# A two-layer hybrid decoder step: shared weight tiles, the convolution's halo in one go, roots on GpSimd, and an earlier q

## The chip, the cores and the metric

The kernel runs on one core of one Trainium2 chip. A core has five engines, each with its own queue that it works through in order: TensorE (PE, matmuls), VectorE (DVE), ScalarE (ACT), GpSimd (POOL) and SyncE (SP, which here issues all the DMAs). They wait for each other by semaphores. The metric is the device time of one launch in microseconds. The kernel before took 2385.9 us, the median of three runs (2383.13 to 2389.49).

## The reference

Each of two layers normalises its input, projects it by one weight matrix of 1024 x 2824, runs two groups of heads on the result, and adds the output projection of both to the input. It does so for a prompt of 2048 new tokens and for eight short samples of 4 tokens with caches.

```python
q = _rope(_rms(aq.reshape(B, L, ATT_HEADS, HEAD_DIM), q_norm_g), pos)     # 8 heads of 64
k = _rope(_rms(ak...), pos)                                               # 2 heads
att = _swa_banded(q, k, v, sinks)              # window of 128, softmax with a sink
att = att * jax.nn.silu(ag)
# delta branch: causal convolution over 4 tokens, 1536 channels
xx = jnp.concatenate([conv_buf, dqkv], 1)
y = silu(sum(xx[:, j:j + L] * conv_w[j] for j in range(4)))
q, k = _l2n(q) * 128 ** -0.5, _l2n(k)          # 4 heads of 128
beta, g = sigmoid(db), -exp(a_log) * softplus(da + dt_bias)
o, s_new = _gated_delta(q, k, v, beta, g, s0)  # per chunk: a triangular solve, then a scan
o = _rms(o, dn_norm_g) * jax.nn.silu(dg)
y = jnp.einsum('ble,ed->bld', jnp.concatenate([att, dn], -1), w_out)
return x + y, nk, nv, nbuf, ns
```

`_rms` and `_l2n` each need a reciprocal root of a sum of squares; the convolution needs the last three columns of the tokens before (the halo).

## The kernel before

**Tiling.** A layer is worked in four groups of 512 tokens (gi = 0 to 3), some 297 us each. A group runs all input projections as matmuls of 128 x 512 outputs, in blocks of four or eight weight pieces, one after the other in program order: k/v/gates, the delta branch's k (four tiles), attention q, delta q (four tiles), delta v (four tiles), the gates, then the output projection. Each product is done as three passes over halves (hi and lo) of weights and activations; all these matmuls are line L484.

**Weights.** In group 0 of a layer each piece comes in whole (`raw`, 128 x 512, from a ring of three slots), ACT writes its rounded half hi (L262), POOL the rest lo (L263), and SP stores both to DRAM; groups 1 to 3 load these. In group 0, and for the output weights in group 2, PE also multiplies the samples' rows by the raw piece (L519). The ring of split weights `hl` has five slots.

**Side tasks.** Everything else is a task, cut into steps, with a start and an end counted in projection steps: the table W. While a group's projections are written out, the tasks that are due put their steps in between: k's norm (`k1`), the q heads (`q0`, `q1`), the inversion of the triangular blocks on POOL (`ir0`, `ir1`: `inv_rows`, 31 rounds of L811 and L813, two instructions each), what follows from it on PE (`iv0`, `iv1`), attention (`att0`, `att1`), the delta scan (`sc0`, `sc1`), the samples' attention and delta (`sa`, `sp`, `sh`, in group 1). A scheduler then orders the instructions on each engine; within an engine they start in that order.

**Shared buffers.** Tiles of 4 KB a partition come from five slots (`f4`): among them the two q heads `qh`, the squares, At (the inversion's input, read back from DRAM by L805), X, and the scores Pt. Tiles of 2 KB come from nine slots (`f2`): th of each silu, the inversion's pr and Xh, PT, the output rows. A tile that takes a slot waits until the last reader of the tile before is done.

**q, attention.** L389 to L403 square, sum, take the root, multiply and rotate each of the two `qh`; L645 transposes them on PE, L649 and L650 split the result into q; L668 and L669 multiply by k; L672 (ACT) copies the product into Pt, L673 masks it; L689 is the exponential, L696 the normalisation, L701 the transposition of Pt on PE, L711 the product with v. L681 to L692 are the small steps between.

**Roots.** `rsqrt(out, x)` is a bit trick and three Newton steps on DVE: 11 small instructions (L200, L201, three times L203, L204, L205), on tiles of at most 128 x 16. It is called for x (xrs), k and the q heads (qr), the delta branch's k (sqvk) and q (rq), and its outputs (ro), and for the samples.

**Convolution.** `conv_tile` has one of 12 feature tiles (k, q, v) in a PSUM bank: ACT writes the last tap (L741), DVE adds the three others over the columns d to 511 (L744), each followed by the halo's 1 to 3 columns (L745), then copies the last three columns of the bank to `halo` (L746); `silu2` is a tanh on ACT (L210) and a product on DVE (L211). k and q tiles are KQ, v tiles vT, which PE transposes (L912).

Of the kernel before, what the change touches and what calls it, by code (L numbers as in the profile page):

```python
# [10 lines left out]
F32 = mybir.dt.float32  # L11
F32R = mybir.dt.float32r
BF16 = mybir.dt.bfloat16
I32 = mybir.dt.int32
AF = mybir.ActivationFunctionType
ALU = mybir.AluOpType
# [29 lines left out]

W = dict(k1=8, pre0=13, pre1=19, q0=17, q1=30, ir0=20, ir1=((32,) + (27,) * 3), iv0=(36, 31, 31, 31), iv1=(41, 36, 36, 36), att0=24, att1=47,
         qk0=29, qk1=35, sc0=(41,) * 4, sc1=52, sa0=-4, sa1=30, sp0=20, sp1=50, sh0=58, shd=11, shl=13, wla=4, wraw=3, xn0=2, xn1=8, sla=3,
         md0=53, md1=55, ma0=45)
# [92 lines left out]
def hybrid_kernel(ctx, tc, a):  # L142
# [23 lines left out]
    def f2(shape, dt=F32, name="f2"):  # L166
        return f2p.tile(shape, dt, tag="f2", name=name, bufs=9)

# [9 lines left out]
    def smt(shape, nm, bufs=2):  # L178
        return sm.tile(shape, F32, tag=nm, name=nm, bufs=bufs)
# [11 lines left out]
    trib, selb = tsb[:, 0:P], tsb[:, P:]  # L191
    cs_s = cp.tile([R3, S_END], F32, name="cs_s")
    junk = cp.tile([P, P], BF16, name="junk")
    negc = cp.tile([P, 1], F32, name="negc")

    def rsqrt(out, x):

        n, m = x.shape
        t = sm.tile([P, 16], F32, tag="rs_t", name="rs_t", bufs=2)[:n, :m]
        V.tensor_scalar(t.bitcast(I32), x.bitcast(I32), 1, None, op0=ALU.logical_shift_right)  # L200
        V.tensor_scalar(out.bitcast(I32), t.bitcast(I32), -1, 0x5F3759DF, op0=ALU.mult, op1=ALU.add)  # L201
        for _ in range(3):
            V.scalar_tensor_tensor(t, out, -0.5, x, op0=ALU.mult, op1=ALU.mult)  # L203
            V.tensor_mul(t, t, out)  # L204
            V.scalar_tensor_tensor(out, t, 1.5, out, op0=ALU.add, op1=ALU.mult)  # L205

# [40 lines left out]
    def fetch(first=False):  # L247


        while len(wready) < W["wla"]:  # L250
# [4 lines left out]
            with nullcontext() if first else tc.high_priority():  # L255
                raw = None
                if whole:
                    raw = wp.tile([P, kk, m], F32, tag="raw", name="raw", bufs=W["wraw"])
                    dma(raw, src)
                hl = wp.tile([P, 2, kk, m], F32R, tag="hl", name="hl", bufs=W["wla"] + 1)  # L260
                if split:
                    A.copy(hl[:, 0], raw)  # L262
                    G.tensor_sub(hl[:, 1], raw, hl[:, 0].bitcast(F32))  # L263
                else:
                    dma(hl.bitcast(F32), half)
# [276 lines left out]
    def group(L, gi, xT, sg):  # L542
# [11 lines left out]
        if gi > 0:  # L554
            V.tensor_copy(kT[:, :, 0:P], kT[:, :, NT * P:].bitcast(F32))
        vts = [L.vt]
        kall = f2([P, NT, 2, HD], name="kall")
# [182 lines left out]
        def conv_tile(ft, ps, dest):  # L740
            A.activation(dest, ps, AF.Copy, scale=convw[:, ft, 3:4])  # L741
            for d in range(1, 4):
                w = convw[:, ft, 3 - d:4 - d]
                V.scalar_tensor_tensor(dest[:, d:], ps[:, 0:T - d], w, dest[:, d:], op0=ALU.mult, op1=ALU.add)  # L744
                V.scalar_tensor_tensor(dest[:, 0:d], halo[:, ft, 3 - d:3], w, dest[:, 0:d], op0=ALU.mult, op1=ALU.add)  # L745
            V.tensor_copy(halo[:, ft, :], ps[:, T - 3:T])  # L746
            silu2(dest, dest, P, T)
# [513 lines left out]
    def sample_head(L, h):  # L1261
# [8 lines left out]
        dma(dg, zs[:, Z_DG + h * P:Z_DG + (h + 1) * P])  # L1270
        sel = f2([P, 2, P], name="sel")
        dma(sel, a["const_k"])
        yield
# [91 lines left out]
    dma(cst[:, P:], a["const"][:, P:])  # L1365
    dma(cs_s, a["const_s"])
    V.tensor_copy(identb, ident)
    tsf = f2([P, P + 16], name="tsf")
# [91 lines left out]
```

## Time and profile before

| | us |
|---|---|
| median of 3 runs | 2385.9 (2383.13 to 2389.49) |
| the profiled execution's own time | 2384.89 |
| its span in the trace | 2383.1 |
| PE busy | 2227.7 (93%), 14340 instructions |
| DVE busy | 1642.2 (69%), 5060 instructions |
| ACT busy | 909.6 (38%), 2864 instructions |
| POOL busy | 447.4 (19%), 732 instructions |
| mean granted TensorE clock | 0.972 of full |

A row of the profile names the line, engine and operation, the tile written and the tiles read (KQ<-mm,pc), the size, and behind it the time; "<-" behind an idle time names what ended it. PE rows are at full speed at a granted clock of 1.0 (2.4 GHz) and half of that at 0.5.

### The profile page before, as it was taken

How to read it: one execution, taken by the hardware profiler on the slowest of the kernel's cores; microseconds unless marked ns; L12 is line 12 of the kernel's file. 1: busy time of each engine (PE TensorE's matmuls, PEld its weight loads, DVE VectorE, ACT ScalarE, POOL GpSimd, SP SyncE). 2: the span in 40 equal slices, each digit the busy share in tenths (PEclk: the TensorE clock that was granted, in tenths of full speed). 3: DMA queues.
4: the chain of work that ended last, by engine and by line, in shares of the span. 5: the costliest groups of instructions: out<-in, count | busy, mean ns of one | idle time of the engine just before them, and what ended most of it. 6: DMA issues, size and time to landing. Idle time of an engine off the chain costs nothing.

```text
span 2383.1 us, 41057 instructions
## 1 busy us (share of the span) xinstructions
PE 2227.7 (93%) x14340; PEld 1771.6 (74%) x14340; DVE 1642.2 (69%) x5060; ACT 909.6 (38%) x2864; POOL 447.4 (19%) x732
## 2 busy tenths in 40 slices
PE   6989999879999899979999899999899989999799
PEld 5766788658887687867877677887688777788677
DVE  6677677577678764677656867778767787557663
ACT  3544523234233342334325445244432344323331
POOL 3272320400004000040023623104000130002100
PEclk9989999979999999989999999999999999999899
DMA  5654685514765348544566546854357534675236
GB/s 172 208 190 160 206 282 184 158 57 140 225 194 170 105 146 267 181 124 131 162 213 222 173 148 215 272 190 125 118 162 224 192 113 133 200 231 161 82 116 199
DMA packets 211298, 414.14 MB, mean 174 GB/s; under 512 B 61340, under 2 KB 89604, under 8 KB 211028
## 3 DMA queue, kind: packets, MB, share of 16 engines
q1 hardware_dynamic: 211092, 411.53, 53.4%
q8 instruction: 113, 1.85, 0.3%
q14 instruction: 93, 0.76, 0.1%
HBM read 312.84 MB, written 101.62 MB: 174 GB/s over the span
## 4 chain that ended last, share of the span: by engine, by line
PE 59%; DVE 8%; POOL 6%; DMA 3%; issue 2%; ACT 2%; SPq 0%; POOLq 0%; ACTq 0%; DVEq 0%
PE mm L484 40%; POOL Xh L813 3%; POOL pr L811 3%; PE px L711 2%; PE px L946 1%; PE px L954 1%; PE px L940 1%; PE px L926 1%; PE px L934 1%; PE px L701 1%; PE px L781 1%; DMA hl<-hl 1%; PE px L668 1%; PE px L519 1%; DVE vT L744 1%
## 5 line engine op out<-in xcount | busy, mean ns | idle before, releaser
L484 PE MATMUL mm<-xT,hl 128*128 128x512 f32 x3072 | 777.5, 403 | 4.1 <-POOL hl L263 3.8
L484 PEld LDWEIGHTS mm<-xT,hl 128*128 128x128 f32 x3072 | 571.0, 192 | 124.2 <-issue 6.7
L484 PE MATMUL mm<-hl,xT 128*128 128x512 f32 (+1 forms) x2304 | 511.2, 369 | 44.3 <-DVE rs_t L204 25.9
L484 PEld LDWEIGHTS mm<-hl,xT 128*128 128x128 f32 x2304 | 379.1, 192 | 114.4 <-issue 56.5
L263 POOL TENSOR_TENSOR hl<-raw,hl 128x512 fp32r<-128x512 f32 (+1 forms) x144 | 186.5, 1300 | 409.7 <-ACT hl L262 360.2
L811 POOL TENSOR_TENSOR pr<-At,Xh 128x126 f32<-128x126 f32 (+22 forms) x248 | 99.2, 400 | 580.1 <-DMA At<-ad 286.6
L484 PE MATMUL mm<-mixA,hl 128*128 128x512 f32 x768 | 187.9, 397 | 0.0
L484 PE MATMUL mm<-mixD,hl 128*128 128x512 f32 x768 | 181.6, 392 | 1.0 <-DVE mixD L970 1.0
L1029 POOL TENSOR_TENSOR mixA<-m,mixA 128x256 fp32r<-128x256 f32 x64 | 45.5, 736 | 719.2 <-ACT mixA L1028 492.7
L484 PEld LDWEIGHTS mm<-mixD,hl 128*128 128x128 f32 x768 | 142.6, 188 | 33.7 <-DVE mixD L970 1.8
L744 DVE SCALAR_TENSOR_TENSOR KQ<-mm,pc,KQ 128x511 f32<-128x511 f32 (+2 forms) x192 | 142.0, 740 | 35.1 <-ACT KQ L741 34.8
L484 PEld LDWEIGHTS mm<-mixA,hl 128*128 128x128 f32 x768 | 140.7, 188 | 30.4 <-issue 2.2
L262 ACT CAST hl<-raw 128x512 fp32r<-128x512 f32 (+1 forms) x144 | 85.0, 595 | 140.2 <-PE mm L484 76.4
L689 ACT ACTIVATE Pt<-Pt,nm 128x128 f32<-128x128 f32 x256 | 99.3, 391 | 21.5 <-DVE nm L681 21.5
L813 POOL TENSOR_TENSOR Xh<-Xh,pr 128x126 f32<-128x126 f32 (+22 forms) x248 | 103.0, 416 | 18.9
L1060 DVE TENSOR_TENSOR xr<-mm,xr 128x512 f32<-128x512 f32 x64 | 43.7, 691 | 79.6 <-PE mm L484 79.6
L672 ACT COPY Pt<-px 128x256 f32<-128x256 f32 x128 | 43.7, 374 | 143.1 <-PE px L669 110.8
L704 DVE TENSOR_TENSOR PT<-px,cst 128x512 f32<-128x512 f32 x124 | 82.1, 683 | 16.7 <-PE px L701 16.2
L701 PE MATMUL px<-cst,Pt 128*128 128x128 f32 x256 | 41.9, 289 | 41.2 <-ACT th L210 26.9
L741 ACT ACTIVATE KQ<-mm,pc 128x512 f32<-128x512 f32 x64 | 43.7, 687 | 94.0 <-PE mm L484 93.9
L668 PE MATMUL px<-kT,q 128*128 128x256 f32 (+1 forms) x256 | 72.6, 313 | 5.0 <-DVE q L650 1.7
L359 ACT CAST xT<-x 128x512 fp32r<-128x512 f32 x64 | 35.5, 618 | 93.9 <-PE mm L484 83.0
(392 smaller groups left out, 3708.7 us busy)
## 6 DMA issues: line engine op xcount, KB each, us to landing
hl<-hl SPq DMA_DIRECT2D x512, 512.0 KB
hl<-hl SPq DMA_DIRECT2D x64, 264.0 KB
raw<-in_wf_dram SPq DMA_DIRECT2D x64, 256.0 KB
raw<-in_w_out_dram SPq DMA_DIRECT2D x64, 256.0 KB
x<-in_x_prompt_dram SPq DMA_DIRECT2D x16, 512.0 KB
raw<-in_wt_dram SPq DMA_DIRECT2D x32, 256.0 KB
xr<-in_x_prompt_dram SPq DMA_DIRECT2D x32, 256.0 KB
y<-xr SPq DMA_DIRECT2D x32, 256.0 KB
```

Source lines behind the costliest of these rows:

```text
L262: A.copy(hl[:, 0], raw)
L263: G.tensor_sub(hl[:, 1], raw, hl[:, 0].bitcast(F32))
L484: PE.matmul(pss[u], lhs, rhs, start=(k == 0 and q == 0), stop=(k == 7 and q == 2))
L668: PE.matmul(sps[kv][:, jj, c0:], q, kT[:, kv, cols], start=True, stop=False)
L689: A.activation(Pt[:, kv, j], Pt[:, kv, j], AF.Exp, bias=nm[:, h:h + 1], scale=0.125, accum_out=den[:, h:h + 1])
L701: PE.transpose(pt[:, j, :], Pt[:, kv, j], ident)
L704: V.tensor_mul(ptt, pt, (umat if kb else slower).unsqueeze(1).to_broadcast([P, 4, P]))
L711: PE.matmul(po[kv * HD:kv * HD + HD, :], vts[tt + kb][:, kv * HD:kv * HD + HD], PT[kv, kb].rearrange("p a b -> p (a b)"), start=(kb == 0 o ...
L744: V.scalar_tensor_tensor(dest[:, d:], ps[:, 0:T - d], w, dest[:, d:], op0=ALU.mult, op1=ALU.add)
L811: G.tensor_mul(pr, At[:, j, j + 1:].unsqueeze(2).to_broadcast([P, n, m]), Xh[:, j, 0:m].unsqueeze(1).to_broadcast([P, n, m]))
L813: G.tensor_sub(Xh[:, j + 1:, 0:m], Xh[:, j + 1:, 0:m], pr)
L1029: G.tensor_sub(lo, m, hi.bitcast(F32))
```

## The change

Five edits.

- `raw` comes from the f2 ring. It has 12 slots now, and the ring of three raw slots is gone: the same memory.
- `rsqrt` is one GpSimd instruction, x to the power of -0.5, with a constant tile of -0.5 as its second operand.
- The halo's part of the convolution: at the start of a group (not of group 0, where the halo is zero) five small GpSimd instructions work out, for all twelve tiles, what the halo adds to the first three columns (`hc`); a tile's L745 three times becomes one DVE addition (L751). The copy of the last three columns is done by ACT (L749).
- q0, q1 go from 17, 30 to 18, 27: the q heads' six steps start one projection step later and end three sooner.
- The samples' constant `sel` is loaded once, in place of eight loads into an f2 tile.

```diff
-W = dict(k1=8, pre0=13, pre1=19, q0=17, q1=30, ir0=20, ir1=((32,) + (27,) * 3), iv0=(36, 31, 31, 31), iv1=(41, 36, 36, 36), att0=24, att1=47,
-         qk0=29, qk1=35, sc0=(41,) * 4, sc1=52, sa0=-4, sa1=30, sp0=20, sp1=50, sh0=58, shd=11, shl=13, wla=4, wraw=3, xn0=2, xn1=8, sla=3,
+W = dict(k1=8, pre0=13, pre1=19, q0=18, q1=27, ir0=20, ir1=((32,) + (27,) * 3), iv0=(36, 31, 31, 31), iv1=(41, 36, 36, 36), att0=24, att1=47,
+         qk0=29, qk1=35, sc0=(41,) * 4, sc1=52, sa0=-4, sa1=30, sp0=20, sp1=50, sh0=58, shd=11, shl=13, wla=4, xn0=2, xn1=8, sla=3,
...
     def f2(shape, dt=F32, name="f2"):
-        return f2p.tile(shape, dt, tag="f2", name=name, bufs=9)
+        return f2p.tile(shape, dt, tag="f2", name=name, bufs=12)
...
+    sel = cp.tile([P, 2, P], F32, name="sel")
+    mhalf = cp.tile([P, 16], F32, name="mhalf")
+    V.memset(mhalf, -0.5)
     def rsqrt(out, x):
         n, m = x.shape
-        t = sm.tile([P, 16], F32, tag="rs_t", name="rs_t", bufs=2)[:n, :m]
-        V.tensor_scalar(t.bitcast(I32), x.bitcast(I32), 1, None, op0=ALU.logical_shift_right)
-        V.tensor_scalar(out.bitcast(I32), t.bitcast(I32), -1, 0x5F3759DF, op0=ALU.mult, op1=ALU.add)
-        for _ in range(3):
-            V.scalar_tensor_tensor(t, out, -0.5, x, op0=ALU.mult, op1=ALU.mult)
-            V.tensor_mul(t, t, out)
-            V.scalar_tensor_tensor(out, t, 1.5, out, op0=ALU.add, op1=ALU.mult)
+        G.tensor_tensor(out, x, mhalf[:n, 0:m], op=ALU.pow)
...
-                    raw = wp.tile([P, kk, m], F32, tag="raw", name="raw", bufs=W["wraw"])
+                    raw = f2([P, kk, m], name="raw")
...
+        if gi > 0:
+            hc, ht = smt([P, 12, 3], "hc", 1), smt([P, 12, 2], "ht", 1)
+            G.tensor_mul(hc, halo, convw[:, :, 0:1].to_broadcast([P, 12, 3]))
+            for d in (2, 1):
+                G.tensor_mul(ht[:, :, 0:d], halo[:, :, 3 - d:], convw[:, :, 3 - d:4 - d].to_broadcast([P, 12, d]))
+                G.tensor_add(hc[:, :, 0:d], hc[:, :, 0:d], ht[:, :, 0:d])
...
         def conv_tile(ft, ps, dest):
             A.activation(dest, ps, AF.Copy, scale=convw[:, ft, 3:4])
             for d in range(1, 4):
-                w = convw[:, ft, 3 - d:4 - d]
-                V.scalar_tensor_tensor(dest[:, d:], ps[:, 0:T - d], w, dest[:, d:], op0=ALU.mult, op1=ALU.add)
-                V.scalar_tensor_tensor(dest[:, 0:d], halo[:, ft, 3 - d:3], w, dest[:, 0:d], op0=ALU.mult, op1=ALU.add)
-            V.tensor_copy(halo[:, ft, :], ps[:, T - 3:T])
+                V.scalar_tensor_tensor(dest[:, d:], ps[:, 0:T - d], convw[:, ft, 3 - d:4 - d], dest[:, d:], op0=ALU.mult,
+                                       op1=ALU.add)
+            A.copy(halo[:, ft, :], ps[:, T - 3:T])
+            if gi > 0:
+                V.tensor_add(dest[:, 0:3], dest[:, 0:3], hc[:, ft])
             silu2(dest, dest, P, T)
```

The order of instructions moves with it. Three places follow; lines of the new kernel have other numbers (L484 is L481, L263 L260, L672 L676, L689 L693, L811 and L813 L816 and L818, L210 L207, L741 L745, L649 L653, L668 and L669 L672 and L673, L701 L705, L893 and L898 L898 and L903, L1193 L1198, L912 L917).

First ACT in the last group of layer 0, where the scores of the third block of 128 tokens are copied into Pt; in brackets the engines (or DMA queues) whose semaphore the instruction waits for. The kernel before:

```order
L741 ACTIVATE KQ<-mm,pc 128x512 [waits PE_49] x2
L649 CAST q<-px 64x4x128 [waits PE_49]
L672 COPY Pt<-px 128x256 [waits DMAHW1_49,DMAHW7_49,PE_49,Pool_49]
L689 ACTIVATE Pt,den<-Pt,nm 128x128 [waits DVE_49]
L684 ACTIVATE es<-es 128x8 [waits DVE_49]
L689 ACTIVATE Pt,den<-Pt,nm 128x128 x7
L210 ACTIVATE th<-KQ 128x512 [waits DVE_49,Activation_49]
```

The new kernel:

```order
L653 CAST q<-px 64x4x128 [waits DVE_49]
L745 ACTIVATE KQ<-mm,pc 128x512 [waits PE_49] x2
L676 COPY Pt<-px 128x256 [waits PE_49] x2
L693 ACTIVATE Pt,den<-Pt,nm 128x128 [waits DVE_49]
L693 ACTIVATE Pt,den<-Pt,nm 128x128
L688 ACTIVATE es<-es 128x8 [waits DVE_49]
L693 ACTIVATE Pt,den<-Pt,nm 128x128 x6
L749 COPY halo<-mm 128x3 [waits DVE_49]
L207 ACTIVATE th<-KQ 128x512 [waits DVE_49,DMAHW5_49,Activation_49,Pool_49]
```

The copy into Pt no longer names POOL; the tanh behind the exponentials does. The q splits (L649, now L653) have moved ahead of the block.

Then PE in the second group of layer 0, around the transposition of the samples' rows (xx<-, L1193, now L1198). The kernel before:

```order
L484 MATMUL mm<-xT,hl 128x512 x7
L668 MATMUL px<-kT,q 128x256
L669 MATMUL px<-kT,q 128x256
L668 MATMUL px<-kT,q 128x256
L669 MATMUL px<-kT,q 128x256
L1193 MATMUL px<-cst,xx 128x56 x4
L701 MATMUL px<-cst,Pt 128x128 x4
L645 MATMUL px<-cst,qh 128x128 x4
...
L701 MATMUL px<-cst,Pt 128x128 x4
L893 MATMUL px<-cst,KQ 128x128 x4
L898 MATMUL px<-KQ 128x128 x4
L484 MATMUL mm<-hl,xT 128x512 x2
```

The new kernel:

```order
L481 MATMUL mm<-xT,hl 128x512 x12
L1198 MATMUL px<-cst,xx 128x56 x4
L481 MATMUL mm<-xT,hl 128x512 x18
L705 MATMUL px<-cst,Pt 128x128 x4
...
L481 MATMUL mm<-xT,hl 128x512 x6
L705 MATMUL px<-cst,Pt 128x128 x4
L898 MATMUL px<-cst,KQ 128x128 x4
L481 MATMUL mm<-xT,hl 128x512 x7
L903 MATMUL px<-KQ 128x128 x4
L481 MATMUL mm<-xT,hl 128x512 x48
L917 MATMUL px<-cst,vT 128x128 x4
L481 MATMUL mm<-xT,hl 128x512 x5
```

Between the samples' transposition and the v tiles the new order has 84 projection matmuls of this kind (18, 6, 7, 48, 5) where there was none; and the q transposition (L645) is no longer among them.

Last POOL in group 0 of layer 0, up to the first steps of the inversion. The kernel before:

```order
L263 TENSOR_TENSOR hl<-raw,hl 128x264 x8
L263 TENSOR_TENSOR hl<-raw,hl 128x512 x24
L811 TENSOR_TENSOR pr<-At,Xh 128x31
L813 TENSOR_TENSOR Xh<-Xh,pr 128x31
```

The new kernel:

```order
L202 TENSOR_TENSOR sqvk<-ssk,mhalf 128x16
L260 TENSOR_TENSOR hl<-raw,hl 128x512 x2
L202 TENSOR_TENSOR qr<-qss,mhalf 128x16 x2
L816 TENSOR_TENSOR pr<-At,Xh 128x31
L818 TENSOR_TENSOR Xh<-Xh,pr 128x31
...
L816 TENSOR_TENSOR pr<-At,Xh 128x100
L818 TENSOR_TENSOR Xh<-Xh,pr 128x25x4
L260 TENSOR_TENSOR hl<-raw,hl 128x512 x2
L816 TENSOR_TENSOR pr<-At,Xh 128x96
```

Two roots of q and the first 14 instructions of the inversion stand ahead of two splits (and others behind them) that stood ahead of it before.

## Rows read from the trace of the kernel before

**Rows 1.** The page: busy time of each engine, share of the span, instructions.
```profile
PE 2227.7 (93%) x14340; PEld 1771.6 (74%) x14340; DVE 1642.2 (69%) x5060; ACT 909.6 (38%) x2864; POOL 447.4 (19%) x732
```

**Rows 2.** What PE waited for: us in total, times, longest.
```profile
PE px L701 <- ACT th L210: 26.9, 2, 13.5
PE mm L484 <- DVE rs_t L204: 25.9, 7, 5.5
PE mm L484 <- issue: 13.2, 3, 8.0
...
PE px L607 <- DVE gx L605: 9.3, 6, 4.4
...
PE px L645 <- DVE qh L403: 5.6, 4, 3.7
...
PE px L344 <- DVE xrs L205: 3.1, 3, 2.4
```

**Rows 3.** Last group, layer 0: ACT, PE in time; stretch with engines' busy us, clock.
```profile
1046.99 0.37 ACT L672 COPY Pt<-px 128x256 f32<-128x256 f32 x1 [13.74 <-POOL pr L811]
...
1053.06 1.09 PE L701 MATMUL px<-cst,Pt 128*128 128x128 f32 x4 [13.47 <-ACT th L210]
...
1040.00:1070.00 30.00, 16.94 (x81) 14.37 (x82) 18.02 (x45) 13.79 (x54) 7.12 (x21) 0.77 0.34 101
```

**Rows 4.** Second group, layer 0: PE in time, and the stretch from 460 to 492.
```profile
444.19 12.74 PE L484 MATMUL mm<-xT,hl 128*128 128x512 f32 x55
...
490.18 1.19 PE L484 MATMUL mm<-hl,xT 128*128 128x512 f32 x2 [7.99 <-issue]
...
460.00:492.00 32.00, 13.66 (x57) 10.25 (x57) 24.17 (x71) 15.12 (x57) 4.64 (x12) 0.61 0.17 46
```

**Rows 5.** DVE by line and form: count, then busy us and mean ns.
```profile
L203 DVE SCALAR_TENSOR_TENSOR rs_t<-ro,so 128x4 f32<-128x4 f32 x96 | 18.4, 192 | 2.1
```

**Rows 6.** DVE in time in a v block: start, us, instruction.
```profile
195.93 0.74 DVE L744 SCALAR_TENSOR_TENSOR vT<-mm,pc,vT 128x511 f32<-128x511 f32 x1
...
196.66 0.21 DVE L745 SCALAR_TENSOR_TENSOR vT<-halo,pc,vT 128x1 f32<-128x1 f32 x1
...
199.54 0.69 DVE L211 SCALAR_TENSOR_TENSOR vT<-th,vT 128x512 f32<-128x512 f32 x1
...
200.90 1.13 DVE L205 SCALAR_TENSOR_TENSOR rq<-rs_t,rq 128x16 f32<-128x16 f32 x1
201.96 1.29 DVE L745 SCALAR_TENSOR_TENSOR vT<-halo,pc,vT 128x1 f32<-128x1 f32 x1
```

**Rows 7.** POOL in time, three stretches: start, us, instruction, idle before.
```profile
118.20 2.73 POOL L263 TENSOR_TENSOR hl<-raw,hl 128x512 fp32r<-128x512 f32 x2 [6.51 <-ACT hl L262]
...
131.64 1.11 POOL L811 TENSOR_TENSOR pr<-At,Xh 128x31 f32<-128x31 f32 x1 [1.11 <-DMA At<-ad]
...
138.72 0.39 POOL L813 TENSOR_TENSOR Xh<-Xh,pr 128x100 f32<-128x100 f32 x1
...
200.73 3.73 POOL L263 TENSOR_TENSOR hl<-raw,hl 128x512 fp32r<-128x512 f32 x3 [20.81 <-issue]
...
1018.12 0.24 POOL L811 TENSOR_TENSOR pr<-At,Xh 128x31 f32<-128x31 f32 x1 [130.01 <-DVE rs_t L203]
```

**Rows 8.** POOL and ACT by line and form: busy us, mean ns, idle before.
```profile
L263 POOL TENSOR_TENSOR hl<-raw,hl 128x512 fp32r<-128x512 f32 x128 | 171.4, 1343 | 333.6 <-ACT hl L262 295.4 <-issue 20.8 <-DMA x<-in_x_prompt_dram 5.7
...
L684 ACT ACTIVATE es<-es 128x8 f32<-128x8 f32 x32 | 6.4, 199 | 1.1 <-DVE es L683 1.0
```

**Rows 9.** DVE, then PE, in time, group 0 of layer 0.
```profile
105.61 1.12 DVE L784 SCALAR_TENSOR_TENSOR AK<-px,cck,AK 128x128 f32<-128x128 f32 x4
...
121.48 3.00 PE L484 MATMUL mm<-xT,hl 128*128 128x512 f32 x12
...
140.81 1.65 PE L484 MATMUL mm<-xT,hl 128*128 128x512 f32 x3 [3.82 <-POOL hl L263]
```

More of the change, by code (lines that the diff above doesn't have):

```diff
@@ L1270, in sample_head @@
         dma(dg, zs[:, Z_DG + h * P:Z_DG + (h + 1) * P])
-        sel = f2([P, 2, P], name="sel")
-        dma(sel, a["const_k"])
         yield
@@ L1366, in hybrid_kernel @@
     dma(cs_s, a["const_s"])
+    dma(sel, a["const_k"])
     V.tensor_copy(identb, ident)
```

## The prediction

> **What bounds the kernel now.** I read the busy shares first [rows 1]. PE works in 2227.7 of 2383.1 us, DVE in 1642.2: the kernel is a long run of matmuls, and what can be won is the 155 us in which PE stands (2383.1 - 2227.7) and the work that it does at the lower clock around those holes. Next I read who PE waits for [rows 2]. The list is short: 26.9 us in two waits, put down to ACT's tanh; 25.9 us in seven waits for DVE, put down to the root's L204; 13.2 us of "issue", 8.0 of it in one hole; 9.3 us for the gates' gx; 5.6 us for the normalised q (qh L403); 3.1 us for the x roots. Holes in other engines are not the bound.
>
> Then I read the two largest places in order of time. In the last group of each layer (1040 to 1070 us in layer 0) PE is busy 16.94 of 30 us at a clock of 0.77, and stands 13.47 us before the transposes of Pt at 1053.06 [rows 3]. Followed back: ACT stood 13.74 us and began a copy into Pt at 1046.99, released by POOL's L811, a step of the triangular inversion. Pt is scores, PE had them long before; the copy waited for *memory*: Pt gets the slot of the five f4 tiles that At holds, and At is read until the inversion is nearly done. Behind this copy stood eight exponentials of the tile before, then DVE's normalisation, then PE. The second place is the second group of layer 0: from 460 to 492 us PE is busy 13.66 of 32 us at a clock of 0.61, with a last hole of 7.99 us at 490.18 [rows 4]. There a piece of prompt attention, the sample rows' attention and the q rotation wait for each other on DVE and ACT, and PE has no long matmuls left to put between, because it ran them just before: 55 in one stretch of 12.74 us.
>
> **The change part by part.** The sum is made against the profiled execution: 2384.89 us, a span of 2383.1 and 1.8 around it, 1.0 below the median of the three timed runs.
>
> *q done sooner (q1 30 to 27).* The q heads' tiles sit in the same five f4 slots. With the four q transposes issued earlier, the slots go round in another order: six of ACT's copies into Pt carried a wait for POOL in the program before, and none does in the new one; the copy that stood 13.74 us now waits for PE alone, and is followed at once by the exponentials. What is late next on ACT is the tanh of a k tile behind them, which now waits for a step of the inversion (its f2 slot); the exponentials that PE needs are in front of it. The inversion takes 28.9 us from 1018.12 [rows 7] to 1046.99 and that tanh's step lies some 21 us in, so ACT may stand some 2.5 us there. I take 13.5 - 2.5 = 11 us of the hole in each layer. PE also worked at the lower clock after the hole: a clock of 0.77 over 30 us is 6.9 us of lost clock [rows 3], most of which fell into the hole itself; I take a third of it, 2.4 us, as lying on matmuls. Together 13.4 per layer, -27. Bounds: all of it, -32; and a hole that only moves, -10.
>
> In the second group the built order moves long matmuls in between: 18 after the sample transposes (L1193, now L1198), then 6, 7, 48 and 5 behind the transposes and k products where none stood, 84 in all. At 12.74 / 55 = 0.232 us each [rows 4] that is 19.5 us of PE work placed in holes that sum to 18.3 us (32 - 13.7). It is not new work, it was in front of the holes before; but then the chains on ACT and DVE run beside it. The cover is about as long as the holes, and fits each of them badly; in return the matmuls of these 32 us no longer run at a clock of 0.61. I take -16. Bounds: -24 (18.3 and what the clock costs the 13.7 us of work at most, 0.39 x 13.7 = 5.3) and 0, if the chain is simply as late as before.
>
> *Roots on GpSimd.* 98 roots of 11 DVE instructions each go: 1078 instructions at 0.19 to 0.23 us (the commonest form of L203: 192 ns) [rows 5], about 200 us of DVE's 1642. In their place stand 98 instructions on POOL whose price no row shows. Nearest rows: a two-input step of the inversion with 31 columns takes 0.24 us [rows 7], and the widest thing that POOL does at all, a split of 128x512, 1.34 us [rows 8]. A power is more than a product, its 4 to 16 columns are fewer. I take 0.5 us with its two hand-overs, between 0.24 and 1.34, nearer to the small row since the operand is small. The time where PE waited on a chain that holds a root is in [rows 2]: seven waits of 25.9 us in all (the v tiles' convolution, in which the root's steps sit between the convolution's steps on DVE), four for qh, six for gx. In the v block at 196 us [rows 6] the first tile's three long steps (0.74 each) start at 195.93, and its tanh product at 199.54, 3.6 us later where the three long ones alone take some 2.2; the rest is the short L745, L746 and root steps between them. I take 1 us off each of the seven, 3 off the four qh waits, 1 off the six gx waits together, and 3 back, for places where DVE now stands until POOL has done the root: -8. Bounds: -16, and +10 at 1.34 us and POOL busy with a split when the root comes.
>
> The trace also shows what a busy POOL does to DVE: at 200.90 and 201.96 two DVE steps that take 0.17 to 0.21 elsewhere in the block took 1.13 and 1.29 us, beside three splits on POOL from 200.73 on [rows 6, 7]. The Trainium skill ("SBUF — State Buffer", section "SBUF: two separate sides") has the rule for it: the pair of ports that GpSimd shares with VectorE is an exclusive lock, held for a whole instruction, and a VectorE step with two SBUF inputs waits it out. This row agrees. By that rule each root on POOL holds such a step up for as long as it takes, at 0.5 us 98 x 0.5 = 49 us of DVE at most (an estimate); DVE keeps some 150 us of what it was given back, so the sum would stay as it is.
>
> *Halo.* Per tile three short DVE steps (L745, 0.21 where nothing holds them up) [rows 6] and one copy go, 288 + 96 in the 96 tiles; 72 adds come, at about the same 0.2, and 30 small steps on POOL at the start of a group, in front of nothing that is due. The copy of the last three columns goes to ACT, 96 x 0.2 us by L684 [rows 8], and now comes behind DVE's last long step, since it reads the bank that these read. Behind it on ACT stands the tanh of the same tile, which waited for DVE anyway. PE gets that bank back one ACT copy later than the long step's end, as it did one DVE copy later before. On the path I count +1 for the hand-over (0 to +3).
>
> *Whole weights in the f2 tiles.* The three raw slots become three more f2 slots: the same memory. In the groups 1 to 3 this is three slots of slack, worth nothing that the waits name. In the first group of a layer raw pieces and f2 tiles share the ring, so some tanh waits for a split of POOL 25 us back: free by then.
>
> *POOL's order in the first group.* This is where I see a loss. Before, POOL did all 24 wide splits that come ahead of the inversion first (the pair at 118.20 among them), and the inversion from 131.64 on [rows 7]. Now the two roots of q and seven rounds of the inversion stand in front of that pair. POOL takes in order: until q's sums of squares are there and At has been read back, the splits wait. The last block that At is read from is written by DVE at 106.7 (105.61 + 1.12) [rows 9], q's squares are issued sooner, and At's read stands sooner on SP's queue, so the inversion may start some 12 us earlier, at 119.6. Its 14 steps take 131.64 to 139.1, 7.5 us, and the first split is done at 119.6 + 7.5 + 1.3 = 128.4, where PE takes such a weight up at 121.48 [rows 9]: 7 us late. In return the hole of 3.82 us at 140.81, where PE waits for a split behind the inversion's steps, should go, as these steps are done by then. I take +4 in each layer, +8. Bounds: -4 (that hole goes and nothing comes) and +18 (second rival).
>
> Sum: -27 - 16 - 8 + 1 + 8 = -42, so 2384.9 - 42 = **2343 us**.
>
> **The rivals.** *The power is dear.* If it is a long routine, each of the 20 PE waits that hang on a root (7 + 4 + 6 + 3 for x) grows by what it takes beyond the 2.2 us of the 11 small steps. At p us the loss is 20 x (p - 2.2); it eats the 43 us of the q part from p = 4.4 on. At 6 us the time is 2343 + 8 + 20 x 3.8, some 2427, slower than before. For it: nothing like a power stands in the trace, and POOL needs 1.34 us for a plain subtraction. Against it: 4.4 us is over three times the dearest POOL row, for a thirty-second of the columns.
>
> *POOL is held up in the first groups.* If At lands as late as before (131.64) the pair's first split ends at 139.1 + 1.3 = 140.4, PE stands 19 us behind 121.48 in each layer, and the 3.8 at 140.81 are part of it: some +18 in each, +36 in place of +8, 2371. For it: the in-order rows; against it: what feeds At is there by 106.7 us [rows 9].
>
> *The holes only move.* Pt's copy no longer waits for POOL but its successors do, and the second group's chain is as long as it was: -13, -5, -4, +8, +1 = -13, 2372. For it: the inversion still starts where it did, behind two roots. Against it: PE has cover in the built order at both places.
>
> **How the numbers follow.** The forecast gets 0.62, with a range of its own of 2320 to 2365; the dear power 0.12, the held-up splits 0.10, moved holes 0.16. A measurement of this kernel tells 0.3% or 7 us from no change. Faster than 2378: 0.60 of the forecast, 0.08 of the splits, 0.10 of the moved holes, 0.78; slower: 0.10 of the power, 0.02 of the rest, 0.12; the remaining 0.10 is within 0.3%. For 8 in 10 I go from 2315 (the good bounds of the q part, half of the others) to 2390, which leaves out most of the dear power and little else.
>
> **What would show it.** Right: no 13-us hole of PE in the last groups (at about 1030 and 2170 us then), ACT's copies into Pt waiting for PE only; 460 to 490 us with PE busy over 25 of 32 us at full clock; POOL's root at 0.25 to 1.3 us; DVE's busy time below 1450. Wrong: root rows of several us on POOL with DVE's q multiply or PE waiting for them; PE waiting for POOL's split around 120 and 1310 us for 10 us or more; the hole in the last groups still there with another name on the wait.

## The result, and the profile after

The changed kernel takes 2423.7 us (median of 4 runs, 2423.28 to 2425.86) where the kernel before takes 2387.1 in the same comparison: a ratio of 1.0155, 95% interval 1.0141 to 1.0168. It is slower by 37 us. The forecast was 2343 us with a range of 2315 to 2390.

The busy times, the line of the page that answers [rows 1]:

```profile
PE 2245.4 (93%) x14340; PEld 1781.6 (73%) x14340; DVE 1439.0 (59%) x3671; ACT 917.9 (38%) x2960; POOL 598.1 (25%) x860
```

DVE has lost 203 us of work (130 of them are the roots', since e1 below, which has the roots back on DVE, stands at 1569.0; the prediction had about 200 for them). POOL has gained 151, and PE stands longer (2424.1 - 2245.4 = 179 us, 155 before). What PE waited for, against [rows 2]:

```profile
PE mm L481 <- ACT halo L749: 37.5, 10, 6.9
PE px L649 <- DVE qh L400: 17.7, 4, 4.5
PE px L516 <- DMA raw<-in_wf_dram: 15.0, 12, 6.1
...
PE px L611 <- DVE gx L609: 10.5, 6, 2.5
...
PE px L341 <- POOL xrs L202: 2.0, 3, 1.3
```

The two waits of 13.5 us for ACT's tanh are gone. The waits for the ends of the v tiles (put down to the halo copy now, to the root then) went from 25.9 to 37.5 us, those for the q heads from 5.6 to 17.7, and waits for raw weights, 1.4 us in all before, are new. The two large places, the last group and the second group of layer 0 in their new positions, against the stretches of [rows 3, 4] (us of the stretch, PE, PEld, DVE, ACT, POOL busy, clock, DMA share, GB/s):

```profile
1046.00:1076.00 30.00, 29.03 (x156) 24.31 (x155) 26.89 (x57) 17.89 (x68) 22.24 (x52) 1.00 0.31 96
478.00:510.00 32.00, 31.57 (x224) 25.82 (x224) 26.67 (x74) 14.33 (x63) 1.84 (x5) 1.00 0.58 172
```

PE is busy 29.0 of 30 us (16.9 before) and 31.6 of 32 (13.7 before), both at the full clock. The gain that the forecast counted on is there in these stretches. It is given back elsewhere, a few us at a time, some of it in the same groups: the last group of layer 0 takes 274.2 us before and after. The power on POOL, by form of its tile (count, then busy us and mean ns, then the idle time of POOL before it):

```profile
L202 POOL TENSOR_TENSOR qr<-qss,mhalf 128x16 f32<-128x16 f32 x16 | 46.1, 2900 | 46.1 <-DVE qss L389 46.1
...
L202 POOL TENSOR_TENSOR ro<-so,mhalf 128x4 f32<-128x4 f32 x32 | 32.6, 1019 | 322.3 <-DVE so L437 280.0 <-DVE nsink L298 39.2 <-PE px L516 1.6
...
L202 POOL TENSOR_TENSOR qr<-qss,mhalf 128x8 f32<-128x8 f32 x8 | 13.1, 1642 | 141.0 <-DVE qss L389 121.8 <-DVE sx L423 19.1
...
L202 POOL TENSOR_TENSOR ro<-so,mhalf 32x1 f32<-32x1 f32 x8 | 4.4, 549 | 205.9 <-DVE so L437 205.9
```

It costs by the column: 0.55 us for one, 1.02 for four, 1.64 for eight, 2.90 for sixteen, that is (2.90 - 1.02) / 12 = 0.157 us a column and 0.39 us besides. And DVE stands behind it (us in total, times, longest):

```profile
DVE ro L440 <- POOL ro L202: 42.3, 38, 2.2
DVE qh L392 <- POOL qr L202: 34.3, 16, 2.9
DVE sqvk L797 <- POOL sqvk L202: 22.4, 8, 2.8
DVE rq L448 <- POOL rq L202: 21.0, 10, 2.4
DVE kall L392 <- POOL qr L202: 11.9, 8, 1.7
```

With three smaller rows this is 139 us in which DVE waits, in order, with everything else that it has to do behind the waiting multiply. The q heads of the last group show one such place; first DVE, then POOL and PE:

```profile
1031.35 0.29 DVE L389 TENSOR_SCALAR qss<-qss 128x16 f32<-128x16 f32 x2
1034.53 1.23 DVE L392 TENSOR_TENSOR qh<-qh,qr 128x1024 f32<-128x1024 f32 x1 [2.88 <-POOL qr L202]
1037.39 1.23 DVE L392 TENSOR_TENSOR qh<-qh,qr 128x1024 f32<-128x1024 f32 x1 [1.63 <-POOL qr L202]
...
1031.59 5.76 POOL L202 TENSOR_TENSOR qr<-qss,mhalf 128x16 f32<-128x16 f32 x2 [5.99 <-DVE qss L389]
...
1040.08 0.69 PE L649 MATMUL px<-cst,qh 128*128 128x128 f32 x2 [4.51 <-DVE qh L400]
```

Both sums are there at 1031.6; the two powers stand one behind the other on POOL for 5.76 us, DVE does nothing else in 4.5 of them, and PE stands 4.51 us before the q transposes. While it runs, the multiply at 1034.53 is not slowed by POOL: it has two inputs from SBUF, runs wholly beside the second power (which ends at 1031.59 + 5.76 = 1037.35), and takes 1.23 us, as the one at 1037.39 does with no power beside it.

### The profile page after: what moved, and what is told of

The parts are those of the page before. It is cut to its first block, busy times and chain, and to the rows that moved or that the text cites. A ratio compares the mean times of both kernels' runs of the same rounds, so it can differ in the third digit from the quotient of the medians.

```text
span 2424.1 us, 39962 instructions
## 1 busy us (share of the span) xinstructions
PE 2245.4 (93%) x14340; PEld 1781.6 (73%) x14340; DVE 1439.0 (59%) x3671; ACT 917.9 (38%) x2960; POOL 598.1 (25%) x860
## 4 chain that ended last, share of the span: by engine, by line
PE 61%; DVE 10%; POOL 9%; DMA 8%; issue 7%; ACT 4%; SPq 1%; POOLq 0%; ACTq 0%; DVEq 0%
PE mm L481 42%; DMA raw<-in_wf_dram 3%; PE px L715 2%; POOL hl L260 2%; POOL Xh L818 2%; POOL pr L816 2%; DMA raw<-in_w_out_dram 2%; POOL qr L202 1%; PE px L516 1%; PE px L786 1%; PE px L945 1%; POOL rq L202 1%; DMA Xd<-xd 1%; PE px L672 1%; PE px L951 1%
## 5 line engine op out<-in xcount | busy, mean ns | idle before, releaser
L481 PE MATMUL mm<-xT,hl 128*128 128x512 f32 x3072 | 784.9, 406 | 9.4 <-POOL hl L260 5.0
L481 PEld LDWEIGHTS mm<-xT,hl 128*128 128x128 f32 x3072 | 578.6, 194 | 134.9 <-POOL hl L260 7.0
L481 PE MATMUL mm<-hl,xT 128*128 128x512 f32 (+1 forms) x2304 | 510.0, 369 | 40.8 <-ACT halo L749 37.5
L481 PEld LDWEIGHTS mm<-hl,xT 128*128 128x128 f32 x2304 | 379.6, 192 | 111.1 <-ACT halo L749 41.7
L260 POOL TENSOR_TENSOR hl<-raw,hl 128x512 fp32r<-128x512 f32 (+1 forms) x144 | 178.8, 1258 | 309.7 <-ACT hl L259 253.7
L481 PE MATMUL mm<-mixA,hl 128*128 128x512 f32 x768 | 191.1, 401 | 0.2 <-POOL hl L260 0.2
L481 PE MATMUL mm<-mixD,hl 128*128 128x512 f32 x768 | 183.4, 393 | 0.2 <-DVE mixD L975 0.2
L202 POOL TENSOR_TENSOR ro<-so,mhalf 128x4 f32<-128x4 f32 (+1 forms) x40 | 37.0, 925 | 528.2 <-DVE so L437 485.9
L481 PEld LDWEIGHTS mm<-mixD,hl 128*128 128x128 f32 x768 | 142.2, 188 | 33.4 <-issue 3.6
L481 PEld LDWEIGHTS mm<-mixA,hl 128*128 128x128 f32 x768 | 142.8, 191 | 31.4 <-issue 1.6
L747 DVE SCALAR_TENSOR_TENSOR KQ<-mm,pc,KQ 128x511 f32<-128x511 f32 (+2 forms) x192 | 137.0, 742 | 43.5 <-ACT KQ L745 41.9
L202 POOL TENSOR_TENSOR qr<-qss,mhalf 128x16 f32<-128x16 f32 (+3 forms) x28 | 63.9, 2291 | 195.0 <-DVE qss L389 172.4
L693 ACT ACTIVATE Pt<-Pt,nm 128x128 f32<-128x128 f32 x256 | 99.3, 391 | 26.2 <-DVE nm L685 25.9
L816 POOL TENSOR_TENSOR pr<-At,Xh 128x126 f32<-128x126 f32 (+22 forms) x248 | 93.3, 376 | 48.8 <-DVE Xh L811 30.6
L818 POOL TENSOR_TENSOR Xh<-Xh,pr 128x126 f32<-128x126 f32 (+22 forms) x248 | 99.1, 400 | 18.9
L653 ACT CAST q<-px 64x512 fp32r<-64x512 f32 x64 | 37.1, 580 | 127.6 <-PE px L649 111.0
L676 ACT COPY Pt<-px 128x256 f32<-128x256 f32 x128 | 42.9, 375 | 107.7 <-PE px L673 106.2
L202 POOL TENSOR_TENSOR sqvk<-ssk,mhalf 128x16 f32<-128x16 f32 x8 | 23.2, 2904 | 230.6 <-DVE ssk L770 230.5
L749 ACT COPY halo<-mm 128x3 f32<-128x3 f32 x96 | 15.3, 159 | 170.6 <-DVE vT L747 127.7
```

What stands on the lines that cost most here:

```text
L202: G.tensor_tensor(out, x, mhalf[:n, 0:m], op=ALU.pow)
L481: PE.matmul(pss[u], lhs, rhs, start=(k == 0 and q == 0), stop=(k == 7 and q == 2))
L676: A.copy(s, sps[kv][:, :, P:])
L693: A.activation(Pt[:, kv, j], Pt[:, kv, j], AF.Exp, bias=nm[:, h:h + 1], scale=0.125, accum_out=den[:, h:h + 1])
L747: V.scalar_tensor_tensor(dest[:, d:], ps[:, 0:T - d], convw[:, ft, 3 - d:4 - d], dest[:, d:], op0=ALU.mult, op1=ALU.add)
L816: G.tensor_mul(pr, At[:, j, j + 1:].unsqueeze(2).to_broadcast([P, n, m]), Xh[:, j, 0:m].unsqueeze(1).to_broadcast([P, n, m]))
```

## The experiments

All ratios are to the kernel before, run on the same chip, with the 95% interval.

**e1: the roots back on DVE, all else as changed.**

```diff
-        G.tensor_tensor(out, x, mhalf[:n, 0:m], op=ALU.pow)
+        ... the 11 DVE instructions of the kernel before
```

> The changed kernel with the roots back on DVE (11 small instructions each); everything else of the change stays. Theory A (the dear power alone turns the change round: 2.9 us for 16 columns on POOL, where PE, DVE and SP queue behind it): all other parts together win about what the prediction gave them, so 2335 to 2355 us, and the waits of PE for the q heads (17.7 us in four) and for raw weights (15.0 us in twelve) fall under 8 us each. Theory B (the other parts lose too, the raw pieces in the shared ring or the ACT halo copy above all): 2380 to 2405 us, with these waits still there.

Measured: 2344.9 us, ratio 0.9834 (0.9818 to 0.9851). Theory A: the power alone turns the change round, and is worth 2423.7 - 2344.9 = 79 us by the medians, 77 by the ratios. PE's waits for the q heads fall from 17.7 to 1.3 us; those for raw weights do not fall (16.1 us in fourteen), so that part of the expectation was wrong, they have another cause. The same q heads in e1, on DVE:

```profile
1001.16 0.29 DVE L393 TENSOR_SCALAR qss<-qss 128x16 f32<-128x16 f32 x2
1001.36 0.30 DVE L201 TENSOR_SCALAR rs_t<-qss 128x16 int32<-128x16 int32 x2
...
1003.46 0.29 DVE L206 SCALAR_TENSOR_TENSOR qr<-rs_t,qr 128x16 f32<-128x16 f32 x2
1003.67 2.36 DVE L396 TENSOR_TENSOR qh<-qh,qr 128x1024 f32<-128x1024 f32 x2
```

Here the two chains of 11 steps run through each other (each row is two instructions, x2, one of either head), and both roots are done 2.3 us after the sums, where POOL takes 5.8.

**e2: the power alone, in the kernel before.**

```diff
-        t = sm.tile(...) ... 11 DVE instructions
+        G.tensor_tensor(out, x, mhalf[:n, 0:m], op=ALU.pow)
```

> The kernel before with only the roots moved to POOL's power. Theory A: the power costs what the other parts win and 37 us more, some 80 us, so 2450 to 2480 us. Theory B: the power costs 20 to 40 us, 2405 to 2430 us. If it is less than in the changed kernel because the q heads are less urgent there (q1 of 30), 2400 or under.

Measured: 2472.4 us, 1.0367 (1.0351 to 1.0382): +88 us, as theory A has it. The power costs about the same whether the rest of the change is there or not (79 and 88).

**e3: the power for up to four columns only.**

```diff
+        if m <= 4:
+            G.tensor_tensor(out, x, mhalf[:n, 0:m], op=ALU.pow)
+            return
+        ... the 11 DVE instructions
```

> The changed kernel with the power on POOL only for tiles of up to 4 columns (x, ro and the sample rows; about 1.0 us each in the trace), and the 11 DVE instructions for the wider ones (q heads, k, the delta branch's k and q). Theory A with the price per column as the cause: within 8 us of e1, since 1.0 us is less than the 2.2 us of the DVE chain. Theory A with the hand-over to POOL as the cause, whatever its length: half way back to the changed kernel, 2375 to 2395 us. Theory B: as e1 there, 2380 to 2405 us.

Measured: 2352.3 us, 0.9857 (0.9841 to 0.9874). It is 7 us over e1 by the medians and some 5 by the ratios, whose intervals overlap: the narrow ones cost little if anything, and nearly all of the 79 us hangs on the 42 wide ones. DVE still stands 46.5 us in 38 waits behind the outputs' root ro; at most these few us of it reach the end.

**e4: the q table of before in the changed kernel.**

```diff
-W = dict(k1=8, pre0=13, pre1=19, q0=18, q1=27, ...
+W = dict(k1=8, pre0=13, pre1=19, q0=17, q1=30, ...
```

> The changed kernel with the q table of before (q0 17, q1 30). Theory A: the early q makes PE come to the q transposes before the two powers are done (4 waits of 4.5 us); with the old table these waits shrink by 18 us, but the two 13 us holes of the last groups and the holes of the second group come back, so 2435 to 2460 us. Theory B (the early q itself brings nothing): 2405 to 2424 us.

Measured: 2447.5 us, 1.0259 (1.0244 to 1.0274): the early q gains 24 us even beside the dear power.

**e5: a product in place of the power.** The root's values are left out; the program is the same, instruction for instruction, on every engine.

```diff
-    V.memset(mhalf, -0.5)
+    V.memset(mhalf, 0.01)
...
-        G.tensor_tensor(out, x, mhalf[:n, 0:m], op=ALU.pow)
+        G.tensor_tensor(out, x, mhalf[:n, 0:m], op=ALU.mult)
```

> The changed kernel with the power replaced by a product with 0.01 on POOL: the roots are left out, the instructions stand in the same order on every engine, and only the price of one differs (some 0.2 us where the power takes 0.55 to 2.9). Theory A1 (the time that DVE stands in order behind the power, 139 us in 86 waits, carries the loss): that idle time falls under 30 us and the kernel takes 2325 to 2350 us. Theory A2 (the hand-over to another engine and POOL's queue carry it, whatever the instruction takes): 2385 us or more.

Measured: 2349.6 us, 0.9840 (0.9815 to 0.9864). The product takes 0.18 to 0.22 us (first row), and the waits of DVE for it are down to one large row (us, times, longest); in time, the q heads follow their sums in 0.2 us:

```profile
L202 POOL TENSOR_TENSOR qr<-qss,mhalf 128x16 f32<-128x16 f32 x16 | 3.3, 224 | 63.3 <-DVE qss L389 63.3
```

```profile
DVE ro L440 <- POOL ro L202: 18.9, 26, 5.3
```

```profile
998.18 0.29 DVE L389 TENSOR_SCALAR qss<-qss 128x16 f32<-128x16 f32 x2
998.68 2.37 DVE L392 TENSOR_TENSOR qh<-qh,qr 128x1024 f32<-128x1024 f32 x2 [0.21 <-POOL qr L202]
```

So neither the hand-over to another engine, nor POOL's in-order queue, nor the new order of the instructions makes the loss: the price of the instruction does. Even at the price of a product the roots on POOL win nothing over e1 (0.9840 and 0.9834).

**e6: each power issued twice.**

```diff
         G.tensor_tensor(out, x, mhalf[:n, 0:m], op=ALU.pow)
+        G.tensor_tensor(out, x, mhalf[:n, 0:m], op=ALU.pow)
```

> The changed kernel with each power issued twice in a row, the second with the same result: the price of a root doubles and nothing else changes. Theory A1: the loss grows in proportion to the price, some 79 us for 150 us of powers, so another 75 to 110 us, 2500 to 2535 us. If most of a power is hidden and only a few places count, half of that, 2450 to 2475 us.

Measured: 2559.3 us, 1.0716 (1.0698 to 1.0733), +136 us, more than any expectation. DVE's rows for POOL in this run:

```profile
DVE qh L393 <- POOL qr L203: 81.2, 16, 8.6
DVE ro L441 <- POOL ro L203: 77.5, 40, 2.9
DVE rq L449 <- POOL rq L203: 44.7, 10, 5.4
DVE sqvk L798 <- POOL sqvk L203: 44.7, 8, 5.6
```

With the smaller ones 290 us. By the three doses (e5, changed, e6) the waits of DVE for the root are about 24, 139 and 290 us and the kernel takes 2349.6, 2423.7 and 2559.3: 0.64 us of time for a us of standing at first (74 / 115), then 0.90 (136 / 151). I read this so: the first part of each wait is still covered by matmuls that PE has at hand, and the more it grows, the less is; no run shows this by itself.

How it reaches PE stands in the same three traces. From e5 to the changed kernel the span grows by 74.3 us (2349.8 to 2424.1). PE stands 52.6 us longer (126.1 to 178.7) and works 21.7 us longer on the same 14340 matmuls (2223.7 to 2245.4), with a mean granted clock of 0.969 in place of 0.980. Of its named waits, those at the ends of the v tiles grow by 17.4 us (20.1 to 37.5), those for the q heads appear with 17.7 and those for gx grow by 7.7, all behind DVE's work. The other way, POOL being late with its own splits, is small: PE's wait for them grows by 0.8 us (6.8 to 7.6); only in e6 it reaches 21.0.

**e7: e1 with the raw pieces in a ring of their own.**

```diff
-        return f2p.tile(shape, dt, tag="f2", name=name, bufs=12)
+        return f2p.tile(shape, dt, tag="f2", name=name, bufs=9)
...
-                    raw = f2([P, kk, m], name="raw")
+                    raw = wp.tile([P, kk, m], F32, tag="raw", name="raw", bufs=3)
```

> Kernel e1 (roots on DVE) with the raw pieces in their own ring of three again and nine f2 slots. If the shared ring delays the raw loads (PE waits 16.1 us for them in fourteen waits in e1, in before under 2 us): these waits go and the time is 2330 to 2338 us. If the ring is neutral, as the prediction had it: within 5 us of e1, 2340 to 2350 us.

Measured: 2358.6 us, 0.9876 (0.9857 to 0.9896), slower than e1 by some 10 us (0.0042 of the time). Both expectations were wrong. The waits for raw did go (3.1 us in two), and the first group is 10 us shorter (its 865th projection matmul starts at 341.0 us, at 351.0 in e1). But the holes of the second group are back; the stretch that answers [rows 4], first in e7, then in e1:

```profile
460.00:492.00 32.00, 19.89 (x158) 15.24 (x158) 22.27 (x60) 10.31 (x43) 2.39 (x4) 0.79 0.33 93
```

```profile
460.00:492.00 32.00, 31.66 (x229) 25.23 (x228) 25.57 (x68) 11.48 (x46) 0.00 (x0) 1.00 0.57 177
```

In e7's built order the long matmuls stand in front of the samples' transposition again (65 in a row), as in the kernel before; in e1 they stand between. It is the ring edit that brings the new order there, not the early q. Its two halves, the three more slots and the sharing with the raw pieces, were not run apart.

**e8: the early q alone.** The edit of e4 the other way round, in the kernel before.

> The kernel before with q0 18 and q1 27 and nothing else. The prediction's terms for q alone (27 and 16 us): 2342 us. If the early q needs the DVE time that the other parts give back, or meets the f4 slots in another order without them: 2355 to 2385 us, with one of the large holes still there.

Measured: 2358.3 us, 0.9869 (0.9850 to 0.9888), 30 us less. The holes of the last groups are gone (PE busy 27.15 of the 30 us from 1016), ACT's copies into Pt no longer wait for POOL, but the second group keeps its last hole, and PE is busy 21.13 us of its stretch from 460 to 492 (13.66 before):

```profile
479.95 1.19 PE L484 MATMUL mm<-hl,xT 128*128 128x512 f32 x2 [8.73 <-issue]
```

**e9: the ring alone.** The edit of e7 the other way round, in the kernel before.

> The kernel before with the raw pieces in an f2 ring of twelve and nothing else. The built order has 96 long matmuls between the samples' transposition and the v tiles of the second group, as the changed kernel has, and the six copies into Pt still wait for POOL. Theory C (the ring, not the early q, fills the second group's holes): the 18 us of holes at 460 to 492 go, the 13.5 us holes of the last groups stay, and the first groups lose some 10 us to late raw loads: 2372 to 2382 us. The prediction's account (the ring is worth nothing): 2385 us, within 5.

Measured: 2382.3 us, 0.9981 (0.9972 to 0.9991), 4.5 us less. The time alone does not decide: it is just over theory C's 2372 to 2382 and also within 5 us of the prediction's account. The trace does, and has what theory C asked for: the second group's stretch (at 470 us here) is full, the last groups' waits are all there, and raw weights are waited for.

```profile
470.00:502.00 32.00, 30.32 (x308) 23.41 (x308) 26.87 (x76) 13.08 (x53) 0.00 (x0) 1.00 0.44 130
```

```profile
PE px L701 <- ACT th L210: 26.0, 2, 14.0
...
PE px L519 <- DMA raw<-in_wf_dram: 9.0, 12, 1.9
```

**e10: e1 with the old halo.**

```diff
-        if gi > 0:
-            hc, ht = ... and the five GpSimd instructions that fill hc
...
-            A.copy(halo[:, ft, :], ps[:, T - 3:T])
-            if gi > 0:
-                V.tensor_add(dest[:, 0:3], dest[:, 0:3], hc[:, ft])
...
+                V.scalar_tensor_tensor(dest[:, 0:d], halo[:, ft, 3 - d:3], w, dest[:, 0:d], op0=ALU.mult, op1=ALU.add)
+            V.tensor_copy(halo[:, ft, :], ps[:, T - 3:T])
```

> Kernel e1 (roots on DVE) with the halo's part of the convolution as before: three short DVE steps and a DVE copy per tile, none on ACT and POOL. If the prediction's +1 is right, within 5 us of e1, 2340 to 2350 us; if DVE's time matters, 2350 to 2360 us; if the copy on ACT costs (24.5 us of PE waits name it in e1), 2330 to 2340 us.

Measured: 2359.3 us, 0.9888 (0.9873 to 0.9902): beside the other parts the halo edit is worth some 13 us (0.0054) where the prediction had a loss of 1. The wait of PE at the ends of the v tiles is 21.6 us in six (put down to the root) against 24.5 in twelve (put down to the halo copy), so it isn't won there alone. By the starts of the same projection matmuls, 9.9 of the 11.8 us between the two traces lie in the first groups of the two layers (3.0 and 6.9), where raw pieces share the ring; by which waits I did not settle.

The two edits hang together. e7 is e8 with the halo edit (and the constant `sel` loaded once), on the old ring: 2358.6 and 2358.3 us, 0.9876 and 0.9869, so there the halo edit is worth nothing. e10 is e8 with the new ring (and `sel`) and the old halo: 0.9888 and 0.9869, so there the ring is worth nothing. Both together, e1, are some 8 us better than e8 (0.9834 and 0.9869), with intervals that just touch. The halo edit without the other changes was not run.

**e11: two Newton steps in place of three, on DVE.**

```diff
-        for _ in range(3):
+        for c in (1.50087896, 1.50000057):
             V.scalar_tensor_tensor(t, out, -0.5, x, op0=ALU.mult, op1=ALU.mult)
             V.tensor_mul(t, t, out)
-            V.scalar_tensor_tensor(out, t, 1.5, out, op0=ALU.add, op1=ALU.mult)
+            V.scalar_tensor_tensor(out, t, c, out, op0=ALU.add, op1=ALU.mult)
```

(and 0x5F376908 as the first constant.)

> Kernel e1 with two Newton steps in place of three, with constants fitted for two: 8 DVE instructions a root, 294 fewer in all. If the chain's length shows at the ends of the v blocks and before gx: 0.6 us at some twenty places, 2330 to 2340 us; if other work fills the time between the steps, 2340 to 2348 us.

Measured: 2340.2 us, 0.9805 (0.9789 to 0.9821), the fastest version here; its interval overlaps that of e1 (0.9818 to 0.9851), so the 5 us between the medians are not settled. Both beat the kernel before and the changed one.

## Why the prediction was wrong

**The step that failed: "I take 0.5 us ... between 0.24 and 1.34, nearer to the small row since the operand is small."** The two bounds were rows of other operations, and neither bounds a power. At sixteen columns it takes 2.90 us, over twice the upper bound; the price goes by the column, and small tiles of 16 columns are wide by that measure. The chance of 0.12 for a dear power and the bound of +10 came from this. e5 and e6 show that the price alone decides: at 0.2 us the same program takes 2349.6, at twice the price 2559.3.

**With it failed "3 back, for places where DVE now stands until POOL has done the root".** In the trace DVE stands 139 us there. The root term as a whole, forecast at -8, measures some +79 (e1 to the changed kernel).

**The rival had the right mechanism, by a wrong sum.** It put the turning point at p = 4.4 us and the time at 2427 for 6 us; the kernel took 2423.7 at 2.9 us, so that the two times are near is luck. With the measured 2.9 its own sum gives 20 x 0.7 = 14 us of loss, 2343 + 8 + 14 = 2365, so the price alone does not mend it. What the sum missed is what a root takes DVE away from. It compared p with 2.2 us of chain at 20 places of PE. In the kernel before a chain is 11 short instructions, and others stand between them (two q heads in 2.3 us, e1's rows; the convolution's long steps in [rows 6]). With the power DVE waits in order at the one multiply that needs it, and the q heads' two powers in series take 5.8 us against 2.3. The sum also has no term for the clock: 22 of the 74 us between e5 and the changed kernel are the same matmuls at a lower granted clock.

**The hold-up of DVE beside POOL's roots, "98 x 0.5 = 49 us of DVE at most", does not show.** Of the 22 DVE steps that begin inside a power of 1 us or more and over 0.2 us before its end, none took over 2% more than such a step takes elsewhere, though the estimate has a step with two SBUF inputs, as the q heads' multiply is, wait for the end of the power. DVE's busy time is 1430.0 us in e5, 1439.0 in the changed kernel and 1441.8 in e6, with 143 us more of POOL's work in the second and 163 more again in the third. The stretching that [rows 6, 7] show was beside splits, not beside powers.

The other parts can be read off the time from the first projection matmul of a group to the first of the next (the first group from the start of the span, the last to its end), in us, one profiled execution each:

| | before | e8: q | e9: ring | e7: q, halo | e1: all but the roots | changed |
|---|---|---|---|---|---|---|
| layer 0, first group | 340.4 | 340.1 | 353.3 | 341.0 | 351.0 | 363.7 |
| layer 0, second | 304.8 | 296.0 | 287.0 | 295.1 | 284.2 | 294.5 |
| layer 0, last | 274.2 | 263.5 | 271.7 | 262.0 | 260.6 | 274.2 |
| layer 1, first | 313.0 | 314.4 | 316.1 | 312.5 | 309.5 | 325.6 |
| layer 1, last | 275.5 | 262.5 | 275.4 | 263.9 | 262.7 | 272.3 |

**q done sooner: right.** "13.4 per layer, -27": the last groups are 10.7 and 13.0 us shorter in e8, 13.6 and 12.8 in e1. The holes are gone, and no other wait came in their place. Most of the rest of e8's 30 us lies in the second group.

**The second group: right size, mostly the wrong cause.** "I take -16" stood under the heading of the early q. The ring alone shortens the group by 17.8 us (e9), the early q alone by 8.8 (e8), and all parts together by 20.6 (e1, where PE is busy in 31.7 of 32 us). The matmuls between the samples' transposition and the v tiles came with the ring.

**Whole weights in the f2 tiles: "worth nothing that the waits name" was wrong.** The ring edit moved whole stretches of matmuls in the program's order. In return the first group pays: it ends 12.9 us later in e9, which has nothing but the ring, and 15 us of waits for raw weights stand in the changed kernel (one of 6.07 at 133.85), 9 us in e9. A raw piece now takes a slot in turn with the tiles of all engines. The net of the ring is 4.5 us alone (e9), 10 us beside the other parts (e7 against e1), nothing beside the early q with the old halo (e10 against e8).

**POOL's order in the first group, "+4 in each layer": not seen.** The first group ends 10.6 us later in e1, but it does so with the ring alone (e9), and without the ring it doesn't (e7 and e8). In layer 1 it is 3.5 us shorter. e5 has the prediction's order on POOL, with the roots ahead of the splits, and its first group ends where e1's does (351.5 and 351.0); PE waits for POOL's splits 7.6 us in all in the changed kernel, 3.8 before.

**Halo: "+1".** Beside the old ring that is about what it is (e7 against e8), beside the new one it is some -13 (e10).

Together the parts without the power were forecast at -27 - 16 + 1 + 8 = -34, and e1 gives -40 (2384.9 of its comparison to 2344.9). So the error of the time lies in the root. That the other parts come so near as a sum is partly luck: the first group of layer 0 costs 10.6 us by the ring where the forecast had 4 in each layer by POOL's order, and what the halo and the ring win together was not in it.

## What to carry to other kernels

An operation that the trace does not show has no upper bound in the rows of other operations: where a change hangs on one, forecast both sides of its break-even point, and give the far side a real chance. Work that is cut into many short steps on the engine that needs the result costs less than it looks, since other work runs between; one long instruction elsewhere makes that engine stand in order behind its first use. And a change of a ring of tiles, in its size or in who shares it, can change the program's order: look at what the order does at the holes before you give the credit to another edit, and run the parts with and without each other, since they need not add up.

## What the runs showed of the hardware that I had not expected

The power on GpSimd takes 0.39 us and 0.157 us for each column of a tile (0.55 us for one column, 2.90 us for sixteen), where a product on the same tiles takes 0.18 to 0.22 us, hardly more for sixteen columns than for one. It takes the same in all calls (2.898 to 2.915 us on 128x16). A VectorE step that ran beside such a power was not slowed: none of 22 was, the longest of them 1.23 us, while beside GpSimd's plain subtractions of 128x512 two steps of 0.17 to 0.21 us took 1.13 and 1.29 us [rows 6, 7].
